# Retention head outputs: transposed values moved on two DMA queues in 2 KB runs, split ahead of the rotation, and the sums of x computed before the first gates

## The chip, the cores and the metric

The kernel runs on one core of a Trainium2 chip. The core has five instruction queues that run side by side and wait for each other through semaphores: PE (TensorE, the matmuls), DVE (VectorE), ACT (ScalarE), POOL (GpSimd) and SP (SyncE, which issues DMAs here). ACT issues DMAs too. Each engine takes its instructions strictly in the order in which they stand in its queue, so an instruction that has to wait holds up everything behind it.

The metric is the device time of one execution in microseconds (us). The kernel before takes 1309.05 us, the median of 3 runs (1308.67 to 1309.06).

## The reference

Two layers on a sequence of 512 tokens with 1024 features, all in float32. Layer 0 is a Conformer convolution module, layer 1 is retention, and each is followed by a ConvFFN; a final RMSNorm ends it. Only the retention layer matters here:

```python
def retention(x, positions, w_in, gn_g, w_out):
    h = x @ w_in                                   # 1024 -> 1024 q, 1024 k, 2048 v, 2048 g
    q, k, v, g = split(h)
    q = rotary(q, positions)                       # 4 heads of 256
    k = rotary(k, positions) * 256 ** -0.5
    # per head: o = (q k^T * decay) v              # v: 512 per head
    o = group_norm_per_head(o) * gn_g
    return (silu(g) * o) @ w_out                   # 2048 -> 1024
```

The chunked recurrence of the reference is computed as one causal 512 x 512 score matrix for each head.

## The kernel before

**Precision.** Every matmul operand is split in a high part (a cast on ACT) and a low part (a subtraction on DVE), and each product is three matmuls: high by high, low by high, high by low (`mm3`, lines 268 to 271). Nearly everything that PE multiplies must therefore first pass ACT and then DVE. Tile names end in `h` and `l` for the two parts: `wh` and `wl` are weights (lines 228 and 232), `yt00h` is the high part of piece 0 of head 0's output.

**Weights** come in pieces of 1 MB on SP's queue (line 202, tile `wr`, four buffers). Each piece gives two `wh` and two `wl` tiles, of which there are four each, so the split of a piece waits until PE has finished with the piece two before it.

**Retention** goes head by head, h = 0 to 3. For each head PE computes:

1. `qk`: the projections of q and k, 96 matmuls of 128 x 512 (`ret_qk`);
2. for h > 0, `ro`: the output projection of the head *before* (`proj_out`), 48 matmuls for a group of four 128-row blocks; two groups for h = 1 and 2, one for h = 3;
3. `sc`: the scores of this head (`ret_scores`), 24 matmuls;
4. `vg`: the projections of v and g. Head 0 does them directly in two halves (`ret_vg`), heads 1 to 3 by a scheme of seven half-size block products (`ret_vg_blocks`), which takes sums and differences of blocks of x and of the weights;
5. `o`: scores by v (`ret_o`).

After `o`, DVE takes the statistics of the group norm, ACT applies them (line 1080, `on`), and POOL multiplies the result into the gate (line 1081, `gg`). Now the head's output lies with tokens on the partitions, and `ro` needs it with features there. `ret_t` does this for heads 0 to 2 in two steps: DVE transposes 32 x 32 blocks (line 1090, tile `yq`, four instructions), and `quarters` (lines 388 to 392) moves the blocks between partitions with 16 DMAs of 64 KB into tile `yt`:

```python
def quarters(dst, src, eng):
    for p in range(P // QB):
        for c in range(P // QB):
            eng.dma_start(dst[c * QB:(c + 1) * QB, :, p, :], src[p * QB:(p + 1) * QB, c, :, :])
```

`yt` has the shape [128, 4, 4, 128], indexed by feature block e and token block, so each DMA writes 32 partitions with four runs of 128 floats (512 bytes). `ret_y` then splits the four pieces of `yt` into `yt{h}0h/l` to `yt{h}3h/l` for `ro`.

**The rotation** of q and k (`rs`, lines 955 to 957) multiplies the PSUM results of `qk` by cos and sin on DVE and adds them on POOL; then they are split for `sc`. The tile `rs` and the tile `yq` share one buffer (tag "rs"), so the rotation of a head can start only when the DMAs that read `yq` are done.

**The sums of x** for the block scheme are made by `left_sums(k)` for k = 0 to 3: two normalised blocks of x (line 909, `xn`), four half-size additions (lines 918 to 921, `sa` and `sb`), two casts on ACT (line 924) and two subtractions on DVE (line 925, `sl`). They need only x and its norm, and are used from head 1 on.

**PSUM** has eight banks, given out in turn. A bank is free again when the engine that reads it out has done so: at head 0 the g half of `vg` reuses the banks of `sc`, which DVE reads at line 1053 (`sct`); at head 3 `sc` reuses the banks of `qk`.

**What sets the order.** A scheduler orders the instructions of each engine by its own estimate of when they can run, within the data dependencies; `tc.issue_after(x)` adds the demand that an instruction stands behind x. The order is fixed when the program is built.

Of the kernel before, what the change touches and what calls it, by code (L numbers as in the profile page):

```python
# [9 lines left out]
F32 = mybir.dt.float32  # L10
# [138 lines left out]
def trunk(ctx, tc, xt_d, positions, ret_gn_g, final_g, weights_d, cols_d, mats_d, ident_d, decay_d, invf_d, out):  # L149
# [13 lines left out]
    def psum(name):  # L163
        return pp.tile([P, S], F32, tag="ps", name=name)
# [23 lines left out]
    state = {"emitted": 0, "used": 0}  # L188
    ready = {}

    raws, behind, split_behind = {}, {}, {}
    low_on = {N_CONV - 4: pool}
    latest = [None, None, None]

# [16 lines left out]
    def split_raw(raw, i, unit, ends=None):  # L211
        nk, ncol = descs[i]
        per = 1024 // ncol
        his, los = [], []

        def at(k, c0, c1):
            o = (k % per) * ncol
            return his[k // per][:, o + c0:o + c1], los[k // per][:, o + c0:o + c1]

        for s in range(0, nk * ncol, 1024):  # L220
            hi = wp.tile([P, 1024], F32R, tag="wh", bufs=4, name=f"wh{unit}_{s}")
            lo = wp.tile([P, 1024], F32R, tag="wl", bufs=4, name=f"wl{unit}_{s}")
            his.append(hi)
            los.append(lo)
            ready[unit] = at
            parts = [e - s for e in ends if s < e <= s + 1024] if ends else [1024]
            for o, n in zip([0] + parts, [e - o for o, e in zip([0] + parts, parts)]):
                latest[0] = act.copy(hi[:, o:o + n], raw[:, s + o:s + o + n])  # L228
                with ExitStack() as order:
                    for ins in split_behind.get((i, s), ()):  # L230
                        order.enter_context(tc.issue_after(ins))
                    latest[1] = low_on.get(i, dve).tensor_tensor(out=lo[:, o:o + n], in0=raw[:, s + o:s + o + n],  # L232
                                                                 in1=hi[:, o:o + n].bitcast(F32), op=ALU.subtract)
                yield
# [27 lines left out]
    def weights(ahead=1):  # L262
        i = state["used"]
        weights_ahead(1 + ahead)
        state["used"] += 1
        return ready.pop(i)
# [73 lines left out]
    def split(src, name, tags, hp, gain=None):  # L340
        hi = hp.tile([P, S], F32R, tag=tags[0], name=name + "h")
        lo = hp.tile([P, S], F32R, tag=tags[1], name=name + "l")
        if gain is None:
            latest[0] = act.copy(hi, src)
            latest[1] = dve.tensor_tensor(out=lo, in0=src, in1=hi.bitcast(F32), op=ALU.subtract)
        else:
            latest[0] = act.activation(hi, src, AF.Copy, scale=gain)
            latest[1] = dve.scalar_tensor_tensor(out=lo, in0=src, scalar=gain, in1=hi.bitcast(F32), op0=ALU.mult, op1=ALU.subtract)
        return hi, lo
# [28 lines left out]
    QB = 32  # L378
# [6 lines left out]

        return t.rearrange("p (b a q) -> p a b q", a=NTB, q=QB)

    def quarters(dst, src, eng):

        for p in range(P // QB):  # L390
            for c in range(P // QB):
                eng.dma_start(dst[c * QB:(c + 1) * QB, :, p, :], src[p * QB:(p + 1) * QB, c, :, :])

    def proj_out(ins, name, norm, order=None, between=None, groups=(0, 1)):

# [491 lines left out]
    with ExitStack() as es:  # L887
# [24 lines left out]
        def left_sums(k):  # L912

            x1, x2 = normed(k), normed(k + 4)
            lo, hi = slice(0, N2), slice(N2, S)
            a = xp.tile([P, 2, N2], F32, tag="nacc", bufs=1, name=f"sa{k}")
            b = rt.tile([P, 2, N2], F32, tag="u2", bufs=1, name=f"sb{k}")
            dve.tensor_tensor(out=a[:, 0], in0=x1[:, hi], in1=x2[:, hi], op=ALU.subtract)
            dve.tensor_tensor(out=a[:, 1], in0=a[:, 0], in1=x1[:, lo], op=ALU.subtract)
            dve.tensor_tensor(out=b[:, 0], in0=x1[:, lo], in1=x1[:, hi], op=ALU.subtract)  # L920
            dve.tensor_tensor(out=b[:, 1], in0=x2[:, lo], in1=a[:, 1], op=ALU.add)
            for o, t in ((0, a), (2, b)):
                h, l = (u[:, k, o:o + 2, :] for u in sums)
                act.copy(h, t)
                dve.tensor_tensor(out=l, in0=t, in1=h.bitcast(F32), op=ALU.subtract)
# [9 lines left out]
            t = slice(0, N2) if which[1] == "1" else slice(N2, S)  # L935
            return [tuple(u[:, t] for u in xs[k + (4 if which[2] == "2" else 0)]) for k in range(4)]

        def ret_qk(h):
            qk, pss = [], []
            for part in range(2):  # L940
                w = weights()
                ps = [psum(f"qk{h}{part}{c}") for c in range(2)]
                pss.append(ps)
                for c in range(2):
                    for k in range(KD):
                        mm3(ps[c], *w(k, c * P, (c + 1) * P), *xs[k], k == 0, k == KD - 1)
                    if hooks:
                        hooks.pop(0)()
            rs = rt.tile([P, 5, S], F32, tag="rs", bufs=1, name=f"rs{h}")
            c_, s_ = (cos, sin) if h else rot  # L950
            for part in range(2):
                ps = pss[part]
                for c in range(2):
                    a, b = rs[:, 2 * c, :], rs[:, 2 * c + 1, :]
                    dve.tensor_tensor(out=a, in0=ps[c], in1=c_, op=ALU.mult)
                    dve.tensor_tensor(out=b, in0=ps[1 - c], in1=s_, op=ALU.mult)  # L956
                    pool.tensor_tensor(out=a, in0=a, in1=b, op=ALU.add if c else ALU.subtract)  # L957
                    qk.append(split(a, f"qk{h}{part}{c}", ("qvh", "qvl"), rt6))
            return qk

        def load_gn(h):
            gn = rt.tile([P, DV], F32, tag="gn", bufs=1, name=f"gn{h}")
# [7 lines left out]
        def ret_vg(h, part):  # L970
            res = []
            if part:
                gn = load_gn(h)
                gg = rt.tile([P, NTB, DV], F32, tag="gg", bufs=1, name=f"gg{h}")
            ps = [psum(f"vg{h}{part}{tb}") for tb in range(NTB)]
            for kc in range(2):
                w = weights()
                for tb in range(NTB):
                    for k in range(4):
                        kk = 4 * kc + k  # L980
                        xh, xl = xs[kk]
                        mm3(ps[tb], xh[:, tb * P:(tb + 1) * P], xl[:, tb * P:(tb + 1) * P], *w(k, 0, 512),
                            kk == 0, kk == KD - 1)
            for tb in range(NTB):
                rc = n2.r[:, tb:tb + 1]
                if part == 0:
                    res.append(split(ps[tb], f"v{h}{tb}", ("qvh", "qvl"), rt6, rc))
                else:
                    gated(gg[:, tb, :], ps[tb], gn, scale=rc)
                    res.append(gg[:, tb, :])  # L990
            return res
# [91 lines left out]
        def ret_t(h, gg):  # L1083

            if h == H - 1:
                return gg
            sq = rt.tile([P, 5, S], F32, tag="rs", bufs=1, name=f"yq{h}")[:, :4].rearrange(
                "p c (e i q) -> p c e i q", i=NTB, q=QB)
            for i in range(NTB):
                dve.transpose(sq[:, :, :, i, :].rearrange("p c e q -> p e c q"),  # L1090
                              gg[i].rearrange("p (e c q) -> p e c q", e=4, q=QB))
            yt = rt.tile([P, 4, 4, P], F32, tag="gg", bufs=1, name=f"yt{h}")
            quarters(yt, sq.rearrange("p c e i q -> p c e (i q)"), nc.sync)
            return yt

        def ret_y(h, yt):
            if h == H - 1:
                ys = []
                for e in range(4):
                    ps = psum(f"yt{h}{e}")  # L1100
                    for i in range(NTB):
                        pe.transpose(ps[:, i * P:(i + 1) * P], yt[i][:, e * P:(e + 1) * P], ident)
                    ys.append(split(ps, f"yt{h}{e}", ("yth", "ytl"), rt4))
                return ys
            return [split(yt[:, e].rearrange("p a n -> p (a n)"), f"yt{h}{e}", ("yth", "ytl"), rt4) for e in range(4)]

        qk = ret_qk(0)
        pss = [psum(f"sc0{j}") for j in range(NTB)]
        v = ret_vg(0, 0)
        sc = ret_scores(0, qk, pss)  # L1110
        left_sums(0)
        gg = ret_vg(0, 1)
        left_sums(1)
        ret_o(0, sc, v, gg)
        yt = ret_t(0, gg)
        for k in range(KD):
            normed_split(k)
        for h in range(1, H):
            qk = ret_qk(h)
            if h == 1:  # L1120
                left_sums(2)
                left_sums(3)
            ys = ret_y(h - 1, yt)
            proj_out(ys, f"ro{h - 1}", None, order=by_quarter, groups=(0,) if h == H - 1 else (0, 1))
            sc = ret_scores(h, qk, None)
            v, gg = ret_vg_blocks(h)
            ret_o(h, sc, v, gg)
            yt = ret_t(h, gg)
# [143 lines left out]
```

## Time and profile before

| what | value |
|---|---|
| median of 3 runs | 1309.05 us |
| profiled execution: its time | 1308.67 us |
| profiled execution: span from first to last instruction | 1306.9 us |
| PE busy | 1284.3 us, 98% |
| DVE busy | 810.5 us, 62% |
| ACT busy | 520.5 us, 40% |
| POOL busy | 357.1 us, 27% |
| mean granted TensorE clock | 0.995 |
| retention layer | about 546 to 940 us of the span |

Times in the profile's views are microseconds from the start of the span. In a timeline row the columns are start, duration, engine, line, operation, written tile <- read tiles, sizes, and in brackets the idle time of that engine just before and what ended it. Buffer numbers are left out of names. A duration on DVE and ACT includes the fill and drain that overlaps with the next instruction, so the distance between starts says what an instruction costs in a sequence.

### The profile page before, as it was taken

The numbers are of one execution on the slowest core, as the hardware profiler recorded it, in microseconds if no ns is written. First come the engines' busy times: TensorE is split into PE (matmuls) and PEld (weight loads), VectorE is DVE, ScalarE is ACT, GpSimd is POOL, SyncE is SP. The second block draws the span as 40 slices with busy tenths as digits, with TensorE's granted clock in tenths as the row PEclk, the third lists the DMA queues.
The fourth block names the chain that finished last, engine by engine and source line by source line (L and its number), as shares of the span: only waits on it lengthen the run. The fifth ranks groups of instructions, "written<-read, shape, count | busy, mean of one in ns | idle before, by whom it ended". The sixth has DMA issues, their size and how long they took to land.

```text
span 1306.9 us, 15117 instructions
## 1 busy us (share of the span) xinstructions
PE 1284.3 (98%) x5955; PEld 1068.5 (82%) x5955; DVE 810.5 (62%) x1036; ACT 520.5 (40%) x703; POOL 357.1 (27%) x305
## 2 busy tenths in 40 slices
PE   9999999999999999999699999999999999999997
PEld 7889988888888888888588888788888888888886
DVE  6998657565335554577696596586766553355542
ACT  6646644343114343334335335344533331233332
POOL 0957323787006111122210301314211110011111
PEclk9999999999999999999899999999999999999999
DMA  8533422322222223322304414323224342213011
GB/s 318 231 123 104 146 97 89 105 90 104 97 98 93 100 78 111 118 97 79 103 29 137 137 41 161 105 76 134 70 92 132 99 153 99 97 65 128 34 65 64
DMA packets 40534, 140.48 MB, mean 107 GB/s; under 512 B 10896, under 2 KB 21904, under 8 KB 26384
## 3 DMA queue, kind: packets, MB, share of 16 engines
q1 hardware_dynamic: 38016, 135.59, 30.4%
q10 hardware_dynamic: 2448, 3.94, 0.9%
q8 instruction: 46, 0.75, 0.2%
q14 instruction: 24, 0.20, 0.0%
HBM read 130.08 MB, written 2.10 MB: 101 GB/s over the span
## 4 chain that ended last, share of the span: by engine, by line
PE 90%; DVE 4%; DMA 1%; SPq 1%; issue 1%; POOL 1%; ACT 1%; POOLq 0%; ACTq 0%; DVEq 0%
PE fa L269 6%; PE fu L269 6%; PE fu L270 6%; PE fa L271 6%; PE fa L270 6%; PE fu L271 6%; PE fo L271 3%; PE lo L269 3%; PE fo L269 3%; PE lo L270 3%; PE lo L271 3%; PE fo L270 3%; PE cph L535 2%; PE ro L269 2%; PE ro L270 2%; PE ro L271 2%
## 5 line engine op out<-in xcount | busy, mean ns | idle before, releaser
L232 DVE TENSOR_TENSOR wl<-wr,wh 128x1024 fp32r<-128x1024 f32 (+2 forms) x242 | 301.2, 1247 | 217.8 <-ACT wh L228 210.7
L228 ACT CAST wh<-wr 128x1024 fp32r<-128x1024 f32 (+2 forms) x244 | 250.6, 1029 | 372.3 <-PE fo L271 82.7
L807 POOL MEMSET ap<- 128x2 f32 x44 | 4.2, 100 | 371.3 <-DVE ft L812 334.1
L968 POOL TENSOR_TENSOR gg<-gg,gn 128x512 f32<-128x512 f32 x16 | 27.6, 1726 | 187.4 <-ACT gg L967 187.4
L816 DVE TENSOR_TENSOR fy<-fu,ft 128x512 f32<-128x512 f32 x44 | 30.4, 690 | 69.0 <-PE fu L271 35.4
L810 ACT ACTIVATE ft<-ap,prm 128x512 f32<-128x512 f32 x44 | 35.9, 815 | 70.4 <-DVE ap L808 70.4
L584 DVE SCALAR_TENSOR_TENSOR tp<-hp,prm,tp 128x512 f32<-128x512 f32 x80 | 55.9, 752 | 0.4
L575 POOL TENSOR_TENSOR pla<-pla,plt 128x512 f32<-128x512 f32 x36 | 49.2, 1367 | 9.7 <-ACT pla L571 5.7
L811 DVE SCALAR_TENSOR_TENSOR ft<-ap,prm,ft 128x512 f32<-128x512 f32 x44 | 36.9, 839 | 17.7 <-ACT ft L810 17.5
L813 ACT ACTIVATE ft<-ft 128x512 f32<-128x512 f32 x44 | 27.9, 633 | 45.8 <-DVE ft L812 45.4
L957 POOL TENSOR_TENSOR rs<-rs 128x512 f32<-128x512 f32 x16 | 23.6, 1500 | 69.2 <-DVE rs L956 51.3
L814 POOL TENSOR_TENSOR ft<-ft,n3r 128x512 f32<-128x512 f32 x22 | 32.3, 1467 | 29.1 <-ACT ft L813 29.1
L814 POOL TENSOR_TENSOR ft<-ft,n1r 128x512 f32<-128x512 f32 x22 | 31.5, 1433 | 28.3 <-ACT ft L813 28.3
L812 DVE SCALAR_TENSOR_TENSOR ft<-ap,prm,ft 128x512 f32<-128x512 f32 x44 | 36.1, 820 | 1.5
L574 ACT ACTIVATE plt<-hp,prm 128x512 f32<-128x512 f32 x36 | 25.8, 722 | 20.7 <-POOL pla L575 20.2
L535 PEld LDWEIGHTS cph<-ph,cmat 128*128 128x128 f32 x288 | 32.6, 192 | 0.2
L535 PE MATMUL cph<-ph,cmat 128*128 128x128 f32 x288 | 32.6, 275 | 0.0
L253 DVE TENSOR_TENSOR wr<-wr,wr 128x1024 f32<-128x1024 f32 x24 | 29.7, 1245 | 0.0
L808 DVE TENSOR_TENSOR ap<-fa,n3r 128x512 f32<-128x512 f32 x22 | 15.1, 691 | 20.9 <-PE fa L271 20.9
L426 DVE TENSOR_TENSOR xT<-ro,xT 128x512 f32<-128x512 f32 x32 | 21.4, 684 | 10.1 <-PE ro L271 10.1
L808 DVE TENSOR_TENSOR ap<-fa,n1r 128x512 f32<-128x512 f32 x22 | 15.1, 690 | 17.0 <-PE fa L271 17.0
L852 POOL TENSOR_SCALAR near<-prod 128x512 f32<-128x512 f32 x11 | 23.5, 2136 | 0.9
(1851 smaller groups left out, 3851.8 us busy)
## 6 DMA issues: line engine op xcount, KB each, us to landing
wr<-in_weights_dram SPq DMA_DIRECT2D x106, 1024.0 KB, 4.8
cmat<-in_mats_dram SPq DMA_DIRECT2D x4, 2304.0 KB, 10.9
yt<-yq SPq DMA_DIRECT2D x48, 64.0 KB, 2.1
wr<-in_weights_dram SPq DMA_DIRECT2D x4, 512.0 KB, 3.3
wr<-in_weights_dram SPq DMA_DIRECT2D x6, 256.0 KB, 7.6
xt<-xq SPq DMA_DIRECT2D x32, 48.0 KB, 2.0
xT<-in_xt_dram SPq DMA_DIRECT2D x4, 256.0 KB, 4.6
xT<-in_xt_dram SPq DMA_DIRECT2D x2, 512.0 KB, 8.7
```

What stands on the lines that cost most here:

```text
L228: latest[0] = act.copy(hi[:, o:o + n], raw[:, s + o:s + o + n])
L232: latest[1] = low_on.get(i, dve).tensor_tensor(out=lo[:, o:o + n], in0=raw[:, s + o:s + o + n], in1=hi[:, o:o + n].bitcast(F32), op=ALU.su ...
L269: pe.matmul(ps, wh, xh, start=first, stop=False, **check)
L270: pe.matmul(ps, wl, xh, start=False, stop=False, **check)
L271: pe.matmul(ps, wh, xl, start=False, stop=last, **check)
L535: pe.matmul(ps[:, g * P:(g + 1) * P], mats[i][g][:, s, :], ph[:, g, NSH - 1 - s:NSH - 1 - s + P], start=s == 0, stop=s == NSH - 1)
L575: gate[0] = pool.tensor_tensor(out=pl, in0=pl, in1=tm, op=ALU.add).ins
L584: dve.scalar_tensor_tensor(out=a, in0=hp[:, t:t + S], scalar=tap(t, i), in1=a, op0=ALU.mult, op1=ALU.add)
L810: act.activation(t, ap[:, 2:], AF.Identity, scale=wc(2), bias=wc(3))
L811: dve.scalar_tensor_tensor(out=t, in0=ap[:, 1:1 + S], scalar=wc(1), in1=t, op0=ALU.mult, op1=ALU.add)
L812: dve.scalar_tensor_tensor(out=t, in0=ap[:, 0:S], scalar=wc(0), in1=t, op0=ALU.mult, op1=ALU.add)
L814: scaled = pool.tensor_tensor(out=t, in0=t, in1=norm.rb, op=ALU.mult)
```

## The change

There are four edits.

- `quarters` takes several engines and gives the 16 DMAs to them in turn by c; for the retention layer these are SP and ACT, eight each. `yt` is laid out with the token block outside, so that each DMA writes one run of 2 KB on each of its 32 partitions in place of four of 512 bytes. `split` gets views of the tile that fit this layout.
- The split of `yt` is written inside `ret_qk`, ahead of the rotation. It must stand behind the split of the last weight piece that `ret_qk` asked for; the rotation's multiplications on DVE must stand behind the split of `yt`.
- The split of the next weight piece (ACT's casts and DVE's subtractions) must stand behind the split of `yt`.
- `left_sums(0)` moves ahead of the first head's scores, and `left_sums(1)` to `left_sums(3)` to just behind them, ahead of the g half of `vg`. Before, as the program was written, number 1 stood behind that half, and numbers 2 and 3 behind the `qk` of head 1 (the scheduler had drawn number 1 forward already).

```diff
@@ split_raw
-                latest[0] = act.copy(hi[:, o:o + n], raw[:, s + o:s + o + n])
+                with tc.issue_after(cast_behind[i]) if i in cast_behind else nullcontext():
+                    latest[0] = act.copy(hi[:, o:o + n], raw[:, s + o:s + o + n])
@@ split
-            latest[0] = act.copy(hi, src)
-            latest[1] = dve.tensor_tensor(out=lo, in0=src, in1=hi.bitcast(F32), op=ALU.subtract)
+            to_hi, to_lo = (t.rearrange("p (a n) -> p a n", n=src.shape[2]) if len(src.shape) > 2 else t for t in (hi, lo))
+            latest[0] = act.copy(to_hi, src)
+            latest[1] = dve.tensor_tensor(out=to_lo, in0=src, in1=to_hi.bitcast(F32), op=ALU.subtract)
@@ quarters
-    def quarters(dst, src, eng):
+    def quarters(dst, src, *engs):
...
-                eng.dma_start(dst[c * QB:(c + 1) * QB, :, p, :], src[p * QB:(p + 1) * QB, c, :, :])
+                engs[c % len(engs)].dma_start(dst[c * QB:(c + 1) * QB, :, p, :], src[p * QB:(p + 1) * QB, c, :, :])
@@ ret_qk
-        def ret_qk(h):
+        def ret_qk(h, yt=None):
...
                 w = weights()
+                behind_w = latest[0].ins, latest[1].ins
...
+            with tc.issue_after(behind_w[0]), tc.issue_after(behind_w[1]):
+                ys = ret_y(h - 1, yt) if h else None
+            behind_y = latest[1].ins
+            if h:
+                i, _ = units[state["emitted"]]
+                cast_behind[i] = latest[0].ins
+                split_behind[i, 0] = split_behind[i, 1024] = behind_y,
...
-                    dve.tensor_tensor(out=a, in0=ps[c], in1=c_, op=ALU.mult)
-                    dve.tensor_tensor(out=b, in0=ps[1 - c], in1=s_, op=ALU.mult)
+                    with tc.issue_after(behind_y) if h else nullcontext():
+                        dve.tensor_tensor(out=a, in0=ps[c], in1=c_, op=ALU.mult)
+                        dve.tensor_tensor(out=b, in0=ps[1 - c], in1=s_, op=ALU.mult)
...
-            return qk
+            return qk, ys
@@ ret_t
             yt = rt.tile([P, 4, 4, P], F32, tag="gg", bufs=1, name=f"yt{h}")
-            quarters(yt, sq.rearrange("p c e i q -> p c e (i q)"), nc.sync)
+            yt = yt.rearrange("p b e n -> p e b n")
+            quarters(yt, sq.rearrange("p c e i q -> p c e (i q)"), nc.sync, nc.scalar)
@@ ret_y
-            return [split(yt[:, e].rearrange("p a n -> p (a n)"), f"yt{h}{e}", ("yth", "ytl"), rt4) for e in range(4)]
+            return [split(yt[:, e], f"yt{h}{e}", ("yth", "ytl"), rt4) for e in range(4)]
@@ the retention layer
-        qk = ret_qk(0)
+        qk, _ = ret_qk(0)
         pss = [psum(f"sc0{j}") for j in range(NTB)]
         v = ret_vg(0, 0)
+        left_sums(0)
         sc = ret_scores(0, qk, pss)
-        left_sums(0)
+        for k in range(1, 4):
+            left_sums(k)
         gg = ret_vg(0, 1)
-        left_sums(1)
...
         for h in range(1, H):
-            qk = ret_qk(h)
-            if h == 1:
-                left_sums(2)
-                left_sums(3)
-            ys = ret_y(h - 1, yt)
+            qk, ys = ret_qk(h, yt)
             proj_out(ys, f"ro{h - 1}", None, order=by_quarter, groups=(0,) if h == H - 1 else (0, 1))
```

The scheduler makes its own order of this. Up to sum number 1 of head 0 all queues are as before; POOL's is the same throughout. Three places show what moved. In the changed kernel line numbers are higher: 232 is 233, 253 is 254, 344 and 345 are 346 and 347, 348 is 350, 392 is 394, 426 is 428, 909 is 911, 918 to 921 are 920 to 923, 925 is 927, 955 and 956 are 967 and 968, 1053 is 1065, 1080 is 1092. A number behind a tile's name tells its buffers apart.

ACT at the start of head 1: first the kernel before, from the last `on` of head 0 to the split of `yt`.

```order
L1080 ACTIVATE on_4857<-o_4826,gnb_4846,gr0y 128x512
L228 CAST wh_1024_4996<-wr_4990 128x1024
L228 CAST wh_0_5129<-wr_5127 128x1024
L228 CAST wh_1024_5133<-wr_5127 128x1024
L344 CAST yt00h<-yt_4865 128x512
L344 CAST yt01h<-yt_4865 128x512
```

The same place in the changed kernel:

```order
L1092 ACTIVATE on_4885<-o_4854,gnb_4874,gr0y 128x512
L229 CAST wh_0_5020<-wr_5018 128x1024
L394 DMA yt_4893<-yq_4888 32x512 x8
L229 CAST wh_1024_5024<-wr_5018 128x1024
L346 CAST yt00h<-yt_4893 128x512
L346 CAST yt01h<-yt_4893 128x512
L346 CAST yt02h<-yt_4893 128x512
L346 CAST yt03h<-yt_4893 128x512
L229 CAST wh_0_5129<-wr_5127 128x1024
```

Eight DMAs of `yt` now stand between the two casts of the first `ro` piece (`wr_4990` before, `wr_5018` now), and the casts of the second piece (`wr_5127`) stand behind the casts of `yt`. SP's queue holds the other eight DMAs of `yt`, at head 1 one weight load earlier than it held all 16. On ACT heads 2 and 3 look the same.

DVE around the first read of the scores at head 0 (`sct`), the kernel before:

```order
L232 TENSOR_TENSOR wl_1024_4526<-wr_4519,wh_1024_4525 128x1024
L925 TENSOR_TENSOR sl<-sb_4786,sh 128x512
L232 TENSOR_TENSOR wl_0_4660<-wr_4657,wh_0_4659 128x1024
L232 TENSOR_TENSOR wl_1024_4664<-wr_4657,wh_1024_4663 128x1024
L1053 TENSOR_TENSOR sct_4602<-sc_4453,dm_4593 128x512
```

The changed kernel, from the last `sl` of sum number 2:

```order
L927 TENSOR_TENSOR sl<-sb_4669,sh 128x512
L920 TENSOR_TENSOR sa_4682<-xn_4678,xn_4680 128x256
L922 TENSOR_TENSOR sb_4683<-xn_4678 128x256
L921 TENSOR_TENSOR sa_4682<-sa_4682,xn_4678 128x256
L923 TENSOR_TENSOR sb_4683<-xn_4680,sa_4682 128x256
L233 TENSOR_TENSOR wl_0_4702<-wr_4699,wh_0_4701 128x1024
L911 SCALAR_TENSOR_TENSOR xn_4910<-xT,prm,n2r 128x512
L911 SCALAR_TENSOR_TENSOR xn_4916<-xT,prm,n2r 128x512
L927 TENSOR_TENSOR sl<-sa_4682,sh 128x512
L233 TENSOR_TENSOR wl_1024_4706<-wr_4699,wh_1024_4705 128x1024
L1065 TENSOR_TENSOR sct_4616<-sc_4453,dm_4607 128x512
```

Between the `sl` of sum number 1, which is where both kernels still agree, and `sct`, the changed queue holds eight half-size additions, four `xn` (two for sum 3 and two that the kernel before had already issued earlier, in the place where the changed one makes those of sum 2) and three `sl` more.

DVE at head 3, from the end of the split of `yt` to the last multiplication of the rotation, the kernel before:

```order
L345 TENSOR_TENSOR qk301l<-rs_6526,qk301h 128x512
L253 TENSOR_TENSOR wr_6575<-wr_6575,wr_6577 128x1024
L955 TENSOR_TENSOR rs_6526<-qk_6476,cos 128x512
L956 TENSOR_TENSOR rs_6526<-qk_6476,sin 128x512
L955 TENSOR_TENSOR rs_6526<-qk_6477,cos 128x512
L232 TENSOR_TENSOR wl_0_6702<-wr_6575,wh_0_6701 128x1024
L426 TENSOR_TENSOR xT<-ro_0_6571,xT 128x4x4x32
```

The changed kernel:

```order
L347 TENSOR_TENSOR qk301l<-rs_6542,qk301h 128x512
L428 TENSOR_TENSOR xT<-ro_0_6571,xT 128x4x4x32
L254 TENSOR_TENSOR wr_6575<-wr_6575,wr_6577 128x1024
L428 TENSOR_TENSOR xT<-ro_1_6572,xT 128x4x4x32
L967 TENSOR_TENSOR rs_6542<-qk_6476,cos 128x512
L968 TENSOR_TENSOR rs_6542<-qk_6476,sin 128x512
L428 TENSOR_TENSOR xT<-ro_2_6573,xT 128x4x4x32
L254 TENSOR_TENSOR wr_6577<-wr_6577,wr_6579 128x1024
L428 TENSOR_TENSOR xT<-ro_3_6574,xT 128x4x4x32
L967 TENSOR_TENSOR rs_6542<-qk_6477,cos 128x512
```

The four additions of the `ro` results into x (`xT`), which wait for PE to finish each of four blocks, stood behind the rotation of k and now stand between its three last multiplications. PE's next work behind `ro` is the first matmul of each of the four score blocks, which needs the rotated k and, for the third and fourth, the PSUM banks that these multiplications read.

More of the change, by code (lines that the diff above doesn't have):

```diff
@@ L189, in trunk @@
     ready = {}
-    raws, behind, split_behind = {}, {}, {}
+    raws, behind, split_behind, cast_behind = {}, {}, {}, {}
     low_on = {N_CONV - 4: pool}
```

## The prediction

> **What bounds the kernel now.** I read the page first, then the list of what PE waited for, then the chain and the timelines around the longest wait.
>
> ```profile
> PE 1284.3 (98%) x5955; PEld 1068.5 (82%) x5955; DVE 810.5 (62%) x1036; ACT 520.5 (40%) x703; POOL 357.1 (27%) x305
> ```
>
> ```profile
> PE ro L269 <- ACT yt00h L344: 10.1, 1, 10.1
> PE ro L271 <- DVE yt20l L345: 2.8, 1, 2.8
> ```
>
> PE is the bound: 98% busy, and 1306.9 - 1284.3 = 22.6 us of idle time is all that a new order can win without removing matmuls. Half of that is one wait at head 1, for the first piece of head 0's `yt`. At that wait PE's timeline has these rows:
>
> ```profile
> 637.76 0.39 PE L271 MATMUL qk<-xn7l,wh 128*128 128x512 f32 x1
> ...
> 643.20 0.39 PE L271 MATMUL qk<-xn7l,wh 128*128 128x512 f32 x1
> 653.70 0.79 PE L269 MATMUL ro<-yt00h,wh 128*128 128x512 f32 x1 [10.11 <-ACT yt00h L344]
> ...
> 657.07 0.39 PE L269 MATMUL ro<-yt00h,wh 128*128 128x512 f32 x1
> ```
>
> From 637.76 to 643.20 lie 24 matmuls, so one costs 0.227 us, and `ro` could have begun at 643.43. The matmul at 657.07 is the ninth of `ro`; it should have started at 643.43 + 8 x 0.227 = 645.24. The stall therefore costs **11.8 us**: 10.3 of waiting, and 1.5 because PE comes back slowly (the granted clock over this stage is 0.81):
>
> ```profile
> 643.50:670.00 26.50, 16.39 (x67) 13.37 (x67) 17.13 (x23) 7.82 (x11) 5.52 (x4) 0.81 0.33 94
> ```
>
> The chain of waits says what was late:
>
> ```profile
> 645.59 0.59 SPq L392
> ...
> 650.08 0.60 SPq L392
> 650.73 2.05 DMA yt<-yq
> 653.02 0.63 ACT yt00h L344
> 653.70 0.79 PE ro L269
> ```
>
> SP issues the 16 DMAs of `yt` one after another, the last lands 2.05 us after its issue, and a cast follows. The issuing, not the bytes, takes the time. Ahead of that, the transposes themselves end late at head 1:
>
> ```profile
> 640.90 10.42 SPq L392 DMA_DIRECT2D yt<-yq  x16
> 630.00 5.09 POOL L1081 TENSOR_TENSOR gg<-gg,on 128x512 f32<-128x512 f32 x3 [1.94 <-ACT on L1080]
> 635.35 1.97 POOL L1081 TENSOR_TENSOR gg<-gg,on 128x512 f32<-128x512 f32 x1 [0.26 <-ACT on L1080]
> 640.13 0.69 DVE L1090 STREAM_TRANSPOSE yq<-gg 128x512 f32<-128x512 f32 x1
> 729.28 5.05 POOL L1081 TENSOR_TENSOR gg<-gg,on 128x512 f32<-128x512 f32 x4 [1.09 <-ACT on L1080]
> ```
>
> POOL finishes the last gate product at 637.3, yet the last transpose starts at 640.13: DVE is busy with sums 2 and 3 and weight splits. POOL's four products take 7.3 us here and 5.05 at head 2, where DVE is quiet.
>
> **Head 1: what the change wins.** Sums 2 and 3 leave DVE. About 1.9 us of their work stood ahead of the group-norm factors and 0.9 more between these and the first product, so POOL can begin about 2.8 us earlier, at 627.2; four products at head 2's pace end at 632.3 and the last transpose at 633.0. Each queue then issues eight DMAs. Their price in the new form is not in the trace; the bounds are its 128-descriptor neighbours:
>
> ```profile
> L392 SPq DMA_DIRECT2D yt<-yq x48: 586/599/1141, 640.9 to 838.0; - x48
> L1042 ACTq DMA_DIRECT2D dm<-in_decay_dram x4: 334/334/335, 543.8 to 779.3; - x4
> ```
>
> From 0.33 us (128 runs of 2 KB from memory) to 10.42 / 16 = 0.65 us with the gap (128 runs of 512 bytes between partitions). I take 0.65, since source, destination and partitions stay those of that row. Eight cost 5.2 us; with 2.3 us to land and 0.7 for the cast the first piece is ready at 633.0 + 8.2 = 641.2, before PE wants it at 643.4. The whole 11.8 us are won, with 2.2 us to spare. The split of `yt` and half of the rotation then also run before PE arrives. The second cast of the first `ro` piece now waits behind the eight issues on ACT: ready at 633.0 + 5.2 + 2.3 = 640.5, wanted some 4 us into `ro`, at 647. The second piece's splits, moved behind those of `yt`, end about 2.7 us into `ro` and are wanted 10.9 us (48 matmuls) into it. Both cost nothing.
>
> Head 2 shows no wait although its issue row is as long; its data came just in time, and there the change wins 5 us of slack and no time:
>
> ```profile
> 735.11 10.25 SPq L392 DMA_DIRECT2D yt<-yq  x16
> 746.94 0.62 ACT L344 CAST yt10h<-yt 128x512 fp32r<-128x512 f32 x1 [0.87 <-DMA yt<-yq]
> ```
>
> **Head 0: what the early sums cost.** These are DVE's rows there, and PE's next matmul:
>
> ```profile
> 575.76 1.41 DVE L909 SCALAR_TENSOR_TENSOR xn<-xT,prm,n2r 128x512 f32<-128x512 f32 x2
> 577.09 0.68 DVE L925 TENSOR_TENSOR sl<-sa,sh 128x512 fp32r<-128x512 f32 x1
> 577.69 0.68 DVE L925 TENSOR_TENSOR sl<-sb,sh 128x512 fp32r<-128x512 f32 x1
> 578.29 0.42 DVE L918 TENSOR_TENSOR sa<-xn,xn 128x256 f32<-128x256 f32 x1
> ...
> 579.30 1.22 DVE L232 TENSOR_TENSOR wl<-wr,wh 128x1024 fp32r<-128x1024 f32 x1
> 580.43 0.42 DVE L921 TENSOR_TENSOR sb<-xn,sa 128x256 f32<-128x256 f32 x1
> ...
> 583.83 0.68 DVE L925 TENSOR_TENSOR sl<-sb,sh 128x512 fp32r<-128x512 f32 x1
> 588.97 2.60 DVE L232 TENSOR_TENSOR wl<-wr,wh 128x1024 fp32r<-128x1024 f32 x2 [4.46 <-ACT wh L228]
> 591.48 1.15 DVE L1053 TENSOR_TENSOR sct<-sc,dm 128x512 f32<-128x512 f32 x2
> 593.08 0.40 PE L269 MATMUL vg<-wh,n2x0h 128*128 128x512 f32 x1
> ```
>
> From start to start a pair of `xn` costs 1.33, an `sl` 0.60, a half-size addition 0.34, a `wl` 1.13. DVE has only 4.46 us of idle time here. From 584.43, where the `sl` of sum 1 ends, the changed queue needs eight additions (2.7), four `xn` (2.7), three `sl` (1.8), two `wl` (2.3) and some 0.2 for results that the next instruction needs at once: 584.43 + 9.7 = 594.1. Only then comes `sct`, 0.6 us: 594.7. PE ends the scores at 593.08, and its next matmul reuses the bank that `sct` reads. So PE **loses 1.6 us, with a restart 1.7**. Everything behind, the want at 643.4 included, shifts by as much. Bounds: none if DVE keeps the old pace, 2.9 if one `wl` meets a slow spell. The rest of the scores' work is late too, but `o`, which wants it, starts 21.8 us (96 matmuls) later.
>
> **Head 3.** PE's losses there before:
>
> ```profile
> 840.03 0.39 PE L271 MATMUL qk<-xn7l,wh 128*128 128x512 f32 x1
> ...
> 855.54 0.91 PE L269 MATMUL sc<-qk300h,qk310h 128*128 128x512 f32 x4 [0.43 <-ACT qk310h L344]
> 856.38 0.50 PE L269 MATMUL vg3z<-wh,xn0h 128*128 128x512 f32 x1
> ```
>
> From 840.26 `ro` (48 matmuls, 10.9 us) and four score matmuls (0.6) should have ended at 851.8; `vg3z` starts at 856.4, **4.6 us lost**, 2.8 of them the wait for `yt20l`, which goes. But the rotation of k now stands between the additions of `ro`:
>
> ```profile
> 851.45 1.21 DVE L253 TENSOR_TENSOR wr<-wr,wr 128x1024 f32<-128x1024 f32 x1
> 852.59 0.68 DVE L955 TENSOR_TENSOR rs<-qk,cos 128x512 f32<-128x512 f32 x1
> 854.87 0.62 ACT L344 CAST qk310h<-rs 128x512 fp32r<-128x512 f32 x1 [2.70 <-POOL rs L957]
> 857.88 1.88 DVE L426 TENSOR_TENSOR xT<-ro,xT 128x512 f32<-128x512 f32 x3
> ```
>
> Counted from the start of `ro`: its first block is complete at 7.9 us (34 matmuls), then on DVE an addition (0.6), `wr` (1.1), an addition: 10.2. The two multiplications of the first half of k start there; from them to PE before were 855.54 - 852.59 = 2.95, so the first score matmul could start at 13.2. Two more multiplications and additions, `wr`, and the wait for the fourth block put the last multiplication's end at 14.4, and the fourth score matmul needs its bank. Against 11.4 undisturbed that loses 3.1, with a restart 3.2. Head 3 **wins 4.6 - 3.2 = 1.4 us**. The bounds are 0 lost and, with POOL's pace, 4.5 lost.
>
> **Sum.** 11.8 - 1.7 + 1.4 = 11.5 us less than the profiled execution's 1308.67 (span 1306.9 and 1.8 around it): 1297.2. The median of the runs lies 0.4 above that execution, so **1297.6 us**. Since PE has no other wait to grow into, the later stages follow unchanged.
>
> **Rivals.**
>
> *No new waits (0.18).* The 1.7 and the 3.2 do not come, because DVE's slack suffices or PE's order hides them. For it: both rest on my stacking of instructions that never stood so. Against: every instruction has its row. Gain 11.8 + 4.6 = 16.4, or 14.5 with one of the two: 1292.7 to 1294.5 us.
>
> *The two queues do not overlap (0.15).* If the 16 issues still take 10.4 us between them, the first piece is ready at 634.7 + 10.4 + 3.0 = 648.1 with head 0's shift, PE wants it at 645.1, and 3 us of the gain are lost: 1300.6. No stretch of the trace has both queues issuing, so no row decides. [...]
>
> *Not what it says (0.05).* `yt` comes later still, because the gates or the transposes set the time, and the stall stays in the main: within 2 us of 1309. Against it stands the 10.4 us row of issues.
>
> *Slower (0.06).* ACT is held by its own eight issues and the second cast of each first `ro` piece is late at all three heads. With x us an issue it is ready 8x + 2.3 after the transposes and wanted about 14.5 after; from x = 1.5 on PE waits, and from x = 2.0 the 3 x 8 x 0.5 = 12 us eat the gain; x = 2.2 gives 1297.6 + 3 x 5.4 = 1313.8. The slowest issue of `yt` took 1.14.
>
> **The numbers.** The forecast has 0.56, with a range of its own from 1295.5 to 1299.5. I take 1292.6 to 1302.0 for eight cases in ten: the first rival and most of the second are in it. About 0.2% (2.6 us) can be told from no change. Faster 0.89, same 0.05, slower 0.06.
>
> **What would show it.** Right: no PE wait for `yt00h`; two rows of eight issues near 5 us at head 1, on SP and on ACT; a new PE wait of 1 to 2 us at the first `vg` matmul behind head 0's scores, ended by `sct`; one of 2 to 4 us at head 3's `sc`, ended by DVE's rotation, and none for `yt20l`; an unchanged PE up to 593 us. Wrong: eight issues of 10 us, a wait for a `wh` or `wl` of `ro`, or a wait inside `vg` of heads 1 to 3.

## The result, and the profile after

The changed kernel takes **1296.75 us** (median of 4 runs, 1296.01 to 1297.10) against 1309.05 before; the ratio is 0.9902, 95% interval 0.9885 to 0.9919 (it counts in a fourth run of the kernel before, of 1311.17 us). The forecast was 1297.6 us with a range of 1292.6 to 1302.0. The profiled execution has a span of 1294.2 us, 12.7 less than before.

The busy times of the page and the list of what PE waited for, in the changed kernel:

```profile
PE 1282.1 (99%) x5955; PEld 1068.2 (83%) x5955; DVE 809.4 (63%) x1036; ACT 519.8 (40%) x703; POOL 357.4 (28%) x305
```

```profile
PE sc L270 <- ACT qk310h L346: 1.9, 1, 1.9
PE vg L270 <- DVE sct L1065: 1.7, 1, 1.7
PE warm L171 <- POOL ones L285: 1.0, 1, 1.0
```

The waits for `yt00h` (10.1) and `yt20l` (2.8) are gone; the wait for `sct` is new, and the one for `qk310h` has grown from 0.4 to 1.9. PE does the same 5955 matmuls in both kernels and is idle for 12.1 us instead of 22.6.

Head 1, timeline of ACT, SP, DVE and PE:

```profile
635.75 0.71 DVE L1102 STREAM_TRANSPOSE yq<-gg 128x512 f32<-128x512 f32 x1 [0.54 <-POOL gg L1093]
...
636.50 5.11 ACTq L394 DMA_DIRECT2D yt<-yq  x8
636.54 5.36 SPq L394 DMA_DIRECT2D yt<-yq  x8
...
643.64 0.62 ACT L346 CAST yt00h<-yt 128x512 fp32r<-128x512 f32 x1 [0.94 <-DMA yt<-yq]
...
645.26 0.39 PE L272 MATMUL qk<-xn7l,wh 128*128 128x512 f32 x1
645.48 0.39 PE L270 MATMUL ro<-yt00h,wh 128*128 128x512 f32 x1
```

Both queues issue at the same time, eight DMAs in 5.1 and 5.4 us. The first piece is ready at 644.26, and `ro` follows the last matmul of `qk` after 0.22 us, without a gap.

Head 0, timelines of DVE and PE:

```profile
593.11 1.22 DVE L233 TENSOR_TENSOR wl<-wr,wh 128x1024 fp32r<-128x1024 f32 x1
594.25 0.68 DVE L1065 TENSOR_TENSOR sct<-sc,dm 128x512 f32<-128x512 f32 x1
...
593.12 0.28 PE L272 MATMUL sc<-qk001l,qk011h 128*128 128x256 f32 x1
595.08 0.47 PE L270 MATMUL vg<-wh,n2x0h 128*128 128x512 f32 x1 [1.68 <-DVE sct L1065]
```

Head 3, the same:

```profile
839.76 0.68 DVE L428 TENSOR_TENSOR xT<-ro,xT 128x512 f32<-128x512 f32 x1
840.36 0.68 DVE L967 TENSOR_TENSOR rs<-qk,cos 128x512 f32<-128x512 f32 x1
...
842.43 0.62 ACT L346 CAST qk310h<-rs 128x512 fp32r<-128x512 f32 x1
...
843.10 0.91 PE L270 MATMUL sc<-qk300h,qk310h 128*128 128x512 f32 x4 [1.95 <-ACT qk310h L346]
843.84 0.40 PE L270 MATMUL vg3z<-wh,xn0h 128*128 128x512 f32 x1
...
844.00 0.68 DVE L967 TENSOR_TENSOR rs<-qk,cos 128x512 f32<-128x512 f32 x1
```

Since every kernel here runs the same number of matmuls, the start of the n-th matmul can be compared between two traces, and the steps of the difference show where time was lost. This table gives those steps in us against the changed kernel (plus: slower than it at this place). The columns are the places on PE: head 0 from `sc` to `vg`, head 1 from `qk` into `ro`, the way from there to the end of head 3's `qk`, head 3 from `ro` to `vg`, and all that follows. The first 24 us of the program, which no edit touches, differ by up to 1.1 us between executions and are left out, and so is a step of 0.5 us in `sums_old_load` at 121 us, far ahead of every edit.

| kernel | median us | head 0 | head 1 | to head 3 | head 3 | rest |
|---|---|---|---|---|---|---|
| before | 1309.05 | -1.9 | +11.8 | +0.4 | +2.5 | 0.0 |
| `before_two` | 1307.70 | -1.9 | +11.9 | 0.0 | +0.8 | 0.0 |
| `before_sums` | 1306.00 | +0.1 | +7.8 | +0.4 | +2.3 | 0.0 |
| `one_queue` | 1307.56 | 0.0 | +5.3 | +0.1 | +6.6 | 0.0 |
| `sums_old` | 1303.81 | -1.9 | +11.1 | 0.0 | +1.6 | 0.0 |
| `sums_old_load` | 1300.99 | -1.9 | +8.1 | 0.0 | +1.6 | 0.0 |
| `split_old` | 1299.18 | 0.0 | +2.2 | 0.0 | +1.3 | 0.0 |
| `old_runs` | 1295.03 | 0.0 | 0.0 | 0.0 | 0.0 | 0.0 |
| `both2` | 1292.83 | -1.9 | 0.0 | 0.0 | -2.2 | +1.1 |

### The profile page after: what moved, and what is told of

It is laid out like the page before. It is cut to its first block, busy times and chain, and to the rows that moved or that the text cites. A ratio compares the mean times of both kernels' runs of the same rounds, so it can differ in the third digit from the quotient of the medians.

```text
span 1294.2 us, 15115 instructions
## 1 busy us (share of the span) xinstructions
PE 1282.1 (99%) x5955; PEld 1068.2 (83%) x5955; DVE 809.4 (63%) x1036; ACT 519.8 (40%) x703; POOL 357.4 (28%) x305
## 4 chain that ended last, share of the span: by engine, by line
PE 94%; DVE 3%; issue 1%; DMA 1%; POOL 0%; ACT 0%; POOLq 0%; DVEq 0%
PE fa L270 6%; PE fu L270 6%; PE fa L272 6%; PE fu L272 6%; PE fu L271 6%; PE fa L271 6%; PE lo L272 3%; PE fo L272 3%; PE lo L270 3%; PE fo L270 3%; PE fo L271 3%; PE lo L271 3%; PE cph L537 2%; PE ro L270 2%; PE ro L271 2%; PE ro L272 2%
## 5 line engine op out<-in xcount | busy, mean ns | idle before, releaser
L233 DVE TENSOR_TENSOR wl<-wr,wh 128x1024 fp32r<-128x1024 f32 (+2 forms) x242 | 304.9, 1262 | 207.6 <-ACT wh L229 204.6
L969 POOL TENSOR_TENSOR rs<-rs 128x512 f32<-128x512 f32 x16 | 26.6, 1677 | 72.3 <-DVE rs L968 31.1
```

## The experiments

Each ratio below is to runs of the kernel before that go with it; their medians are 1309.75 us (this part up to `sums_old`), 1309.98 us (`sums_old_load` to `both2`) and 1310.38 us (the last pair).

### One part at a time

`one_queue`, the changed kernel with one queue:

```diff
-            quarters(yt, ..., nc.sync, nc.scalar)
+            quarters(yt, ..., nc.sync)
```

> The changed kernel with all 16 DMAs of yt on SP again, in runs of 2 KB. Theory (the issuing sets when yt is there): at head 1 the issues take 16 x 0.65 = 10.4 us instead of 5.2, so the first piece, ready at 644.3 in the changed kernel, is ready at about 649.6; PE wants it at 645.5 and waits 4.2 us, with a slow restart some 5. At heads 2 and 3 the slack of 4.6 and 3.5 us is used up: waits of about 1 us each, and at head 3 the rotation of k, held behind the later split, costs up to 3 more. Sum 1301.5 to 1306, most likely 1303.5. Rival (the early sums and the split ahead of the rotation brought the gain, the second queue nothing): 1296.8 within 1 us, no wait for yt00h. Second rival (one queue is as fast because runs of 2 KB are issued faster): a row of 16 issues near 5 us, and 1296.8 too.

Measured: 1307.56 us, ratio to before 0.9986 (0.9976 to 0.9995). What PE waited for, and SP's row at head 1:

```profile
PE sc L270 <- ACT qk310h L346: 5.1, 1, 5.1
PE ro L270 <- ACT yt00h L346: 3.5, 1, 3.5
```

```profile
635.71 10.10 SPq L394 DMA_DIRECT2D yt<-yq  x16
```

The 16 issues take 10.1 us on one queue (10.42 with runs of 512 bytes in the kernel before), so runs of 2 KB are not issued markedly faster, and at head 1 the loss is the expected one (5.3). The wait at head 2 did not come (0.1). Head 3 was sized too small: I expected up to 4 there and found 6.6, and the time lies above the expected range. The rotation stands behind the split of `yt` by demand, so a `yt` that comes late delays the rotation and with it the scores. Measured from the end of `qk`, the cast of `yt20h` starts 4.1 us later than in the changed kernel. Of the 6.6 us, 0.7 are lost at the start of `ro`, 3.1 because the wait for `qk310h` is 5.1 us instead of 1.9, and 2.8 behind that wait, where the granted clock (the column ahead of the last two) is 0.55:

```profile
851.00:858.00 7.00, 6.52 (x18) 5.33 (x19) 7.00 (x7) 1.19 (x3) 2.19 (x1) 0.55 0.28 75
```

The early order helps with early data only; with late data it does harm (`before_sums` below, one queue with the old order, loses 2.3 at head 3).

`before_two`, the kernel before with two queues alone:

```diff
-            quarters(yt, ..., nc.sync)
+            quarters(yt, ..., nc.sync, nc.scalar)
```

> The kernel before with one edit: the 16 DMAs of yt alternate between SP and ACT; the layout in runs of 512 bytes, the sums and the order of the splits stay as before. Theory: two rows of eight issues near 5.2 us at head 1; the last transpose stays at about 640.8, so the first piece is ready near 648.8 and PE, which wants it at 643.4, waits about 5.3 us and restarts slowly (6.3 in all instead of 11.8). Head 3 keeps most of its 4.6 us, since the casts of yt stand behind both casts of the next weight piece. About 1303 us (1301.5 to 1305). Rival (two queues alone win everything at head 1): 1297. Rival (the two queues hinder each other, eight issues of 10 us): 1309.

Measured: 1307.70 us, ratio 0.9984 (0.9974 to 0.9993). The expected 1303 was missed; the time is nearest to the second rival's 1309. At head 1 nothing was won (11.9 lost, as before). Head 1 of this kernel:

```profile
639.88 0.33 SPq L202 DMA_DIRECT2D wr<-in_weights_dram  x1
...
640.51 8.23 ACTq L392 DMA_DIRECT2D yt<-yq  x8
640.55 7.91 SPq L392 DMA_DIRECT2D yt<-yq  x8
...
648.85 1.99 ACT L228 CAST wh<-wr 128x1024 fp32r<-128x1024 f32 x2 [12.98 <-DMA yt<-yq]
650.88 0.62 ACT L344 CAST yt00h<-yt 128x512 fp32r<-128x512 f32 x1
```

Eight issues take 8 us here instead of 5.2, and ACT, blocked by its own issues until 648.7, then casts two weight tiles before `yt`. The same issues cost 5.11 and 5.36 us in the changed kernel, so the queues as such don't hinder each other; the row ahead of them is the suspect, a 1 MB weight load 0.6 us earlier. The kernel before has it in the same place.

`before_sums`, the kernel before with the early sums alone:

```diff
+        left_sums(0)
         sc = ret_scores(0, qk, pss)
-        left_sums(0)
+        for k in range(1, 4):
+            left_sums(k)
         gg = ret_vg(0, 1)
-        left_sums(1)
...
-            if h == 1:
-                left_sums(2)
-                left_sums(3)
```

> The kernel before with one edit: the four sums of x stand where the changed kernel has them. Theory: head 0 pays 1.9 us at the first gate matmul (as in the changed kernel); at head 1 the 16 issues on SP start near 636.5, last until 647, the first piece is ready near 649.7 and PE, which wants it at 645.5, waits 4.2 us, with the restart 5. Against before: +1.9 - 6.8 = -4.9, so about 1304 us (1302 to 1306). Rival (the sums alone bring the gain): 1297 to 1299. Rival (they only cost): 1311.

Measured: 1306.00 us, ratio 0.9974 (0.9964 to 0.9984). Head 0 pays the 1.9, head 1 wins 4.0 instead of 6.8: the wait for `yt00h` is 3.7, but 1.9 for `yt00l` follow, because the rotation and a `wl` stand ahead of that split, and nearly 2 us more are lost behind them, where the granted clock is 0.57 (654 to 658 us). This is what the early split is for.

`sums_old`, the changed kernel with the sums in their old place (the diff above, reversed):

> The changed kernel with the sums of x back where the kernel before has them; two queues, 2 KB runs and the early split stay. Theory: the wait for sct at head 0 (1.9 us in all) goes; at head 1 the last transpose is back at about 640.8, the first piece ready near 648.7 against a want at 643.4: a wait of 5.3 us, with the restart 6.3, which is 6.3 more than in the changed kernel. Net about 1301 us (1299.5 to 1302.5). Rival (the early sums buy nothing at head 1, they only cost at head 0): 1294.9.

Measured: 1303.81 us, ratio 0.9958 (0.9943 to 0.9973), 2.8 above the expectation. The transposes end where I put them, but the first piece is ready at 650.7, 3 us after the expected time (648.7, less 1.0 by which this execution is ahead up to there). The chain of waits shows why:

```profile
640.09 5.68 DMA yt<-yq
645.77 0.02 issue
645.80 0.54 ACTq L394
...
647.72 2.12 DMA yt<-yq
...
650.09 0.63 ACT yt00h L346
```

and so does the summary of the line of the DMAs in this stretch (minimum, median, maximum from issue to landing), with the load ahead of them:

```profile
639.42 0.33 SPq L202 DMA_DIRECT2D wr<-in_weights_dram  x1
```

```profile
DMA to landing us min/median/max: 1.9/2.1/5.7
```

The first DMA of `yt` on SP takes 5.7 us to land, and an issue on ACT waits for it. The list of the program's instructions with their waits tells how: the DMAs of this program, whichever queue issues them, take eight semaphores in turn, and from the third on those of `yt` wait until the DMA eight places before has landed. The trace of the kernel before shows the same wait: its load, issued at 640.23, landed at 645.57, and the eighth DMA of `yt`, which waits for it, went out at 645.59. On ACT the first four of `yt` read:

```
L394 DMA yt0_4865<-yq0_4860 32x512 [waits DVE_49]
L394 DMA yt0_4865<-yq0_4860 32x512 [waits DMAHW1_49]
L394 DMA yt0_4865<-yq0_4860 32x512 [waits DMAHW3_49]
L394 DMA yt0_4865<-yq0_4860 32x512 [waits DMAHW5_49]
```

Number 5 is the semaphore of the weight load. So the pair of queues issues seven DMAs and then stands still until the 1 MB has landed (issued at 639.42, 5.7 us to land): the seventh goes out at 642.26 us, the eighth at 645.17.

### The load ahead of the small transfers

`sums_old_load`: as `sums_old`, and the load of weight piece 58 must stand behind head 0's `yt` DMAs.

```diff
+            if h == 0:
+                behind[58] = <the last of these DMAs on SP>
```

> The run with the sums of x back in the old place, and in addition the 1 MB load of the weight piece that stood just ahead of head 0's yt DMAs on SP now stands behind them. In that run (and in the kernel before) this load was issued 0.6 us ahead of the first yt DMA, and no yt DMA on either queue landed before the load had (5.7 us later); the eight issues of each queue took 8 us, not 5.2. Theory (the load in flight holds up the small transfers of both queues): eight issues take 5.2 to 5.4 us, the last lands near 647.4 instead of 649.8, and the wait for yt00h falls from 8.0 us to about 5.6: 1301.2 us (1300 to 1302.5) against 1303.8. Rival (the load has no part; the two queues are slow there for another reason, such as DVE's or POOL's work on the same tiles): issues of 8 us and 1303.8 again. Second rival: the later load makes the weights of a later piece late and the time goes up.

Measured: 1300.99 us, ratio 0.9937 (0.9922 to 0.9951), as the theory had it. Head 1 and the summary of the line:

```profile
640.55 5.10 ACTq L394 DMA_DIRECT2D yt<-yq  x8
640.59 5.34 SPq L394 DMA_DIRECT2D yt<-yq  x8
646.03 0.53 SPq L202 DMA_DIRECT2D wr<-in_weights_dram  x1
```

```profile
DMA to landing us min/median/max: 2.0/2.1/2.3
```

With the load behind them, all 16 land within 2.3 us of their issue, and head 1 loses 3.0 us less. So the early sums give two things at head 1, 8.1 us by letting the transposes end earlier and 3.0 us by putting the small transfers ahead of a load that would hold them up. In the changed kernel the load goes out at 643.99, after them. The trace of `sums_old` shows that the data itself was late, and not only its semaphore. Between 640.0 and 643.7 us seven DMAs of `yt` were issued, but all packets that started were the load's, 8 KB each. In `sums_old_load`, from 640.5 to 643.7 us, all packets were smaller, those of `yt`. What puts the load's packets first was not shown. The line for each stretch, `sums_old` first:

```profile
DMA packets 117, 0.96 MB, mean 259 GB/s; under 512 B 0, under 2 KB 0, under 8 KB 0
```

```profile
DMA packets 266, 0.38 MB, mean 119 GB/s; under 512 B 80, under 2 KB 80, under 8 KB 266
```

### Length of the runs, order of the splits

`old_runs`, the changed kernel with four runs of 512 bytes:

```diff
-            yt = yt.rearrange("p b e n -> p e b n")
```

> The changed kernel with the old layout of yt: each DMA writes four runs of 512 bytes on a partition instead of one of 2 KB. Theory (an issue costs 0.60 to 0.65 us whatever the length of the runs: 0.60 before with 512 bytes, 0.59 to 0.60 after with 2 KB): two rows of eight near 5.2 us, the first piece within 0.3 us of 644.3, 1296.8 within 1 us. Rival (four times as many runs are slower to move or to issue): the last landing more than 1.2 us later, a wait for yt00h, 1298 to 1301.

Measured: 1295.03 us, ratio 0.9892 (0.9875 to 0.9908). ACT's row, against 5.11 us with 2 KB (SP's took 5.21 us against 5.36):

```profile
635.43 5.59 ACTq L394 DMA_DIRECT2D yt<-yq  x8
```

No step of the table differs from the changed kernel by more than 0.04 us; the 1.1 us between the two spans arise in the first 24 us. The 2 KB runs are worth nothing in time here.

`split_old`, the changed kernel with the split of `yt` written behind the rotation, without demands on the order:

```diff
-            with tc.issue_after(behind_w[0]), tc.issue_after(behind_w[1]):
-                ys = ret_y(h - 1, yt) if h else None
...
+            ys = ret_y(h - 1, yt) if h else None
             return qk, ys
```

> The changed kernel without its order of splits: the split of yt is written behind the rotation again, and no instruction is told to stand behind it; two queues, 2 KB runs and early sums stay. The casts of yt then stand behind the first cast of the second weight piece on ACT, which waits for PE until about 2 us before ro. Theory (yt is there so early that the order matters little): the first piece is ready within 0.5 us of PE's want at head 1 (0 to 0.5 us lost), at head 3 the wait for yt20l stays away and the additions of ro stand behind the rotation, so that the score wait of 2.2 us shrinks or stays: 1296 to 1298. Rival (the new order is what took the waits away): waits for yt00h or yt20l of 2 us and more and 1299 to 1302.

Measured: 1299.18 us, ratio 0.9921 (0.9906 to 0.9936), above the theory's range (up to 1298) and just inside the rival's (from 1299). The waits of 2 us and more that the rival named did not come, but shorter ones did. Its waits at head 1 and head 3:

```profile
PE sc L270 <- ACT qk310h L346: 1.7, 1, 1.7
...
PE ro L272 <- DVE yt00l L347: 0.9, 1, 0.9
PE ro L271 <- DVE wl L233: 0.6, 1, 0.6
PE ro L272 <- DVE yt20l L347: 0.5, 1, 0.5
```

The high parts are in time, the low parts just miss. The early split is worth 3.5 us (2.2 and 1.3).

### The two stalls that are left

`both2`: two more demands on the order of the changed kernel, which leave what is computed as it is.

```diff
         sc = ret_scores(0, qk, pss)            # keeps its sct instructions in sct_ins
-        for k in range(1, 4):
+        for k in range(1, 3):
             left_sums(k)
+        with tc.issue_after(sct_ins[1]):
+            left_sums(3)
...
         for k in range(KD):
-            normed_split(k)
+            with tc.issue_after(sct_ins[1]):
+                normed_split(k)
@@ proj_out, for name "ro2"
+                with tc.issue_after(<last multiplication of the rotation>):
                     dve.tensor_tensor(out=dst, in0=src, in1=dst, op=ALU.add)
@@ emit_weights, for units 78 and 79: the additions of raw pieces stand behind the same instruction
```

> The changed kernel with two demands more. (1) Sum number 3 and the normalised blocks for head 1 stand behind the second sct of head 0. (2) At head 3 the additions of ro into x, and the sums of weight pieces 78 and 79, stand behind the last multiplication of the rotation. Theory (each of the two remaining stalls comes from what stands ahead of the awaited instruction on DVE): the wait for sct (1.9 us in all) and the wait for qk310h (2.2 in all) both go, and nothing else is late: 1292.7 us, between 1292.0 and 1294.0. Rival (DVE has too much to do there; what is pushed back becomes late itself): a new wait of 1 to 3 us for xn0l or o at head 0, or for wl of vg3p at head 3, and 1295 to 1298.

Measured: 1292.83 us, ratio 0.9870 (0.9855 to 0.9885). Its DVE and PE at head 0 and at head 3:

```profile
591.49 1.15 DVE L1069 TENSOR_TENSOR sct<-sc,dm 128x512 f32<-128x512 f32 x2
...
835.72 0.67 DVE L969 TENSOR_TENSOR rs<-qk,cos 128x512 f32<-128x512 f32 x1
836.32 1.27 DVE L430 TENSOR_TENSOR xT<-ro,xT 128x512 f32<-128x512 f32 x2
```

```profile
838.71 0.39 PE L273 MATMUL ro<-yt23l,wh 128*128 128x512 f32 x1
838.94 0.80 PE L271 MATMUL sc<-qk300h,qk310h 128*128 128x512 f32 x4
839.57 0.40 PE L271 MATMUL vg3z<-wh,xn0h 128*128 128x512 f32 x1
```

`sct` starts at 591.49 instead of 594.25, and at head 3 the rotation ends before the additions of `ro`. Both stalls are gone, 1.9 and 2.2 us; 1.1 us come back later.

To compare on one chip, the changed kernel and this one ran again together.

> The changed kernel once more, unedited, beside the next run on the same chip: 1296.8 us within 1 us, with the same two PE waits (1.7 us for sct at head 0, 1.9 us for qk310h at head 3). Every account here gives that.

> The kernel with the two further demands (sum 3 behind the second sct of head 0; at head 3 the additions of ro and two weight sums behind the rotation), beside the changed kernel on the same chip. Theory (the two stalls, 1.9 and 2.2 us, were all that these instructions cost): 4.1 us less than the changed kernel in that call up to head 3. The first run lost 1.1 us again behind head 3, 0.3 at the last ro and 0.9 at a wl of the last feed-forward layer: if that is caused by the edits, the difference stays at 3 us and both waits are there again; if it was chance, it is 4.1 us.

Measured: 1295.52 (ratio 0.9893, 0.9875 to 0.9911) and 1292.04 us (0.9863, 0.9848 to 0.9878). The steps of the two traces are again -1.9, -2.2 and +1.1, so the 1.1 us are no chance. They stand at these waits, in both runs of this order:

```profile
PE fu L272 <- DVE wl L233: 0.7, 1, 0.7
PE ro L271 <- ACT yt30h L347: 0.3, 1, 0.3
```

Why the scheduler's order behind head 3 is worse there was not tried. In this pair the version is 3.5 us faster than the changed kernel by the medians, and 3.0 by the steps.

## Why the prediction was right, point by point

- **Head 1, 11.8 us won**: measured 11.8, and the eight issues cost 5.1 and 5.4 against 5.2. The spare was 1.2 us (644.26 against 645.48), not 2.2. With the shift of 2.0 up to there taken off, POOL began at 628.6 and not at 627.2, and the last transpose ended at 634.4 instead of 633.0. The 1.4 us come from head 0: the scheduler put six matmuls of the g half in another order, so that the old blocks of x are used longer. ACT's cast of `xn0h` waits for them and starts at 606.70 instead of 603.28, 1.4 later with the shift off, and all of DVE's later work with it.
- **Right with a step missing.** "Each queue then issues eight DMAs ... 0.65 ... 2.3 us to land" holds only because the weight load moved behind them; to that extent the term came out right by luck. The row of the order showed that the `yt` DMAs stand one load earlier; the prediction gave that no price. Had the load stayed ahead, the price would have been the 3.0 us between `sums_old` and `sums_old_load`, more than the 1.2 us to spare.
- **Head 0, 1.7 us lost**: measured 1.9 by the steps, a wait of 1.68 at the named matmul, with `sct` starting at 594.25 where I had 594.1.
- **Head 3, 4.6 - 3.2 = 1.4 won**: 2.5 won. The step that failed in size is the 3.2; it was 2.2. (The subtraction behind it, 14.4 less 11.4, gives 3.0 and not 3.1.) "The fourth score matmul needs its bank" was wrong: the four score matmuls and even `vg3z` start before the last multiplication at 844.00. The built program gives the third and fourth score block the banks of the first two blocks of `ro`; banks are not given out in strict turn. The rest of the step holds: the first score matmul started 13.0 us after the start of `ro`, where I had 13.2. The sign named for it, a wait of 2 to 4 us ended by DVE's rotation, came as one of 1.95 us ended by ACT's cast of the rotated k.
- **Head 2, no time**: 0.4 won. Before, the first matmuls of head 2's and head 3's `ro` had come late by some tenths in places that I took as undisturbed.
- **Sum**: 11.8 - 1.9 + 2.5 + 0.4 = 12.8 against 12.7 of span; the forecast was 11.5.
- **Rival "no new waits"**: both waits came. Its gain with only one of them should have read 13.2 or 14.7 us, not 14.5. **Rival "not what it says"**: the first piece was ready 1.2 us before PE wanted it. **Rival "the two queues do not overlap"**: refuted by the two rows of 5.1 and 5.4 us at the same time. **Rival "slower"**: its mechanism exists, though not in the changed kernel: with a load ahead, ACT's eight issues block it for 8.2 us (`before_two`).
- **"Since PE has no other wait to grow into"** held; nothing moved behind head 3.

## What to carry to other kernels

Four edits that looked like four gains were one: alone, two queues won 2.1 us and the early sums 3.4 (by the ratios), and each taken out of the whole costs 3.5 to 12 us of span (the low clock behind longer waits included), except the longer runs, which cost and win nothing. A piece of data that is late by three causes in a row is in time only when all are gone, so cost a bundle as a bundle, from the instant at which the consumer wants the data. When small transfers matter, look at what large transfer stands ahead of them in any queue and at the semaphores that the DMAs share. And a demand "A ahead of B" is worth its price only while A's data are early: name what B delays if they are not.

## What the runs showed of the hardware

**Issue price.** A DMA of 64 KB between partitions cost about 0.6 us of the issuing queue (median 0.599 in the kernel before, 0.602 at head 1 of the changed one), with 512-byte and with 2 KB runs alike, though the number of packets of the whole program fell by some 4600 with the longer runs. Two queues paid that price at the same time: eight issues each from 636.50 and 636.54, in 5.11 us on ACT and 5.36 on SP.

**The clock after a short wait.** The same wait at head 3 was followed by a granted clock of 1.00 in the changed kernel and of 0.76 in `sums_old_load`, over 7 us each. First the changed kernel's windows around it, then the other's (the column ahead of the last two is the granted clock):

```profile
842.00:849.00 7.00, 5.90 (x27) 5.00 (x28) 7.00 (x7) 2.00 (x4) 2.60 (x2) 1.00 0.26 75
```

```profile
848.90 1.54 PE L270 MATMUL sc<-qk300h,qk310h 128*128 128x512 f32 x4 [2.03 <-ACT qk310h L346]
```

```profile
848.50:855.50 7.00, 6.60 (x23) 5.53 (x24) 7.00 (x8) 1.56 (x3) 2.20 (x1) 0.76 0.26 73
```

A wait of 1.95 us cost 2.2 us of PE's time, one of 2.03 us cost 3.8. That is the +1.6 of `sums_old` and `sums_old_load` in the table, in which their edits have no part but that they shift the instant of the wait.

The kernel before shows the granted clock at 1.00 up to 646.57, at 0.50 from there to 656.81, and at 1.00 again. In its trace the changes of the clock lie 641.71, 10.24 and 648.53 us apart, in the changed kernel's 1283.41 us, which are 188, 3, 190 and 376 times 3.413 us. Cut these two traces into stretches of that length, from the first record of the clock, and take the ends of matmuls as the profile models them. In the kernel before PE idled for 2.98 us of the stretch from 643.15, and the clock was halved at its end; it idled for 1.64 us of the stretch from 841.13, and the clock stayed full. In the changed kernel the clock stayed full behind 1.68 us of idling (the stretch from 593.19), and a border at 842.36 cut the wait at head 3 into 1.21 and 0.73 us. In `sums_old_load` 0.76 over 7.00 us is 3.4 us at half clock, about one such stretch (an estimate: 0.24 x 7.00 / 0.50). The length of the wait alone does not decide: in `sums_old` it was 1.9 us, and the clock from 850.9 to 858.0 was 0.76 too. So my estimate is that at this place it is chance how a stall falls into the stretches, and for a forecast it means that a stall of 2 us may cost 1.6 us more, as in these two runs, or nothing. How much idling in a stretch halves the clock was not settled.
